# Scan over blocks of 128 tokens: factors of a block in one step, all its matmuls in the next, together with the decay sums of the following block

## The chip, the cores and the metric

The kernel is one program on one core of a Trainium2 chip. The metric is the device time of one execution in microseconds (us). A profile of one execution gives the rows that are shown below; its engines are PE (matmuls; PEld is its weight load), DVE (vector), ACT (activations), POOL (GpSimd) and SP (which issues most DMAs).

## What is computed

The reference is one layer of a hybrid model on 512 tokens of width 1024 and 16 leading meta tokens: two token mixers side by side (gated linear attention, and the state-space scan that is changed here), a gated merge, and a layer of retrieved experts. The scan, cut to what matters:

```
def ssd_chunk_step(S, inp):                       # one chunk of 64 tokens
    xdt, a, Bc, Cc = inp
    acum = jnp.cumsum(a, axis=1)
    seg = jnp.exp(-jnp.abs(acum[:, :, None] - acum[:, None, :]))
    cb = jnp.einsum('btgn,bsgn->btsg', Cc, Bc)
    y = jnp.einsum('btsgr,btsg,bsgrp->btgrp', seg, cb, xdt)
    y = y + jnp.einsum('btgn,bgrpn,btgr->btgrp', Cc, S, jnp.exp(acum))
    to_end = jnp.exp(acum[:, -1:] - acum)
    S = S * jnp.exp(acum[:, -1])[..., None, None] + jnp.einsum('bsgn,bsgr,bsgrp->bgrpn', Bc, to_end, xdt)
    return S, y
...
y = y + d_skip * xs_h;  y = y * jax.nn.silu(z);  y = rmsnorm(y per group of 512 channels)
```

The 2048 channels are four groups of 8 heads of 64. Each group has its own B and C, of 128 states.

## The kernel before

**Tiles.** A group g is scanned by the generator `sscan(g)` in four blocks i = 0 to 3 of 128 tokens, each of two chunks of 64 (A is the state at a block's start, B the state after its first chunk). Tiles are 128 partitions by 512, in float32. In a block the names are: `R`, the decay logarithms spread over a triangle (two POOL instructions); `pr`, their sums on PE (two matmuls); `sgm`, the factors seg times cb times dt, made of pr by DVE (subtract, then drop the sign bit), ACT (exp), DVE (times `cb`) and POOL (times `dt`); `py`, 16 small matmuls of `sgm` with the inputs `xs`; `xw`, the inputs times their decay to the chunk's end; `ssp`, a chunk's addition to the state (one matmul, rows 0 to 63 of `xw` for chunk A, 64 to 127 for B); `sS`, a state (POOL multiplies the old one by its decay, DVE adds `ssp`); `pi`, C times state, one matmul from A into output rows 0 to 63 and one from B into rows 64 to 127; `xd`, the inputs times d, to which DVE adds `py`; `y`, the block's output; `sy`, the sum of its squares (an ACT Square that uses `xd` as its bin); `ry`, the norm's factor (DVE, POOL). `turn` transposes a block's y on PE (`pyt`), copies it on ACT (`yt`) and stores it.

**What runs beside it.** `drive` advances two generators in turn. For g = 0 to 2 the other one is `sproj(g + 1)`, the projections of the next group: six units of 48 matmuls with 264 columns (called BT, CT, x0, x1, x2 and x3 here), each followed by a convolution on DVE (`cv`: four instructions), a tanh on ACT (`silu_t`) and a product on DVE, and then four units of 24 matmuls with 512 columns (z0 to z3). x0 to x3 are also transposed on PE (`px`, `pxm`) and copied by ACT (`xs`, `xsm`). For g = 3 the other one is `gates`, units of 24 matmuls with 512 columns (`pq`). Each unit's weights are split into a high part on ACT (`whi`) and a low part on DVE (`wlo`); three buffers of each rotate, so a split waits until the unit three places earlier is done. `sscan` has nine steps to sproj's ten.

**What sets the order.** The instructions of an engine stand in one row that a scheduler fixes when the program is built; each engine works its row off in that order, and a waiting instruction holds up all behind it. Tiles made by `mps` share four PSUM buffers in rotation: the fifth such tile waits until whoever reads the first has read it.

In PE's row of a group, block 0's matmuls stand behind x0, block 1's behind x2, block 2's behind z0 and block 3's behind z2. Of a block's two steps in the kernel before, the first makes R, pr and sgm up to the exp, and the second all the rest.

Of the kernel before, what the change touches and what calls it, by code (L numbers as in the profile page):

```python
# [6 lines left out]
F32 = mybir.dt.float32  # L7
F32R = mybir.dt.float32r
# [3 lines left out]
AF = mybir.ActivationFunctionType  # L12
OP = mybir.AluOpType
# [8 lines left out]
TT = 4  # L22
HL = L // 2
EPS = 1e-6
# [50 lines left out]
def body(tc, a, out):  # L75
# [3 lines left out]
    def act(o, i, f, **kw):  # L79
        S.activation(out=o, in_=i, func=f, **kw)  # L80

    def tt(eng, o, x, y, op):
        eng.tensor_tensor(o, x, y, op=op)  # L83
# [6 lines left out]
    with ExitStack() as top:  # L90
# [9 lines left out]
        def mps(name):  # L100
            return ps.tile([128, 512], F32, name=name, tag="m")
# [89 lines left out]
        def hv(x, c):  # L191
            return x.rearrange("p (h c) -> p h c", c=c)

        with ExitStack() as mix:
# [99 lines left out]
            def bc(x, g, n=128):  # L294
                return x[:, 8 * g:8 * g + 8, None].to_broadcast([n, 8, 64])
# [39 lines left out]
            def sscan(g):  # L335
                BT, CT, xs, xsm, zt = P_[g]

                p = mps("pcb")
                for i in range(TT):
                    for c in range(2):  # L340
                        t0 = NM + 128 * i + 64 * c
                        T.matmul(p[64 * c:64 * c + 64, 64 * i:64 * i + 64], BT[:, t0:t0 + 64], CT[:, t0:t0 + 64],
                                 start=True, stop=True)
                cb = sg.tile([128, TT, 64], F32, name="cb")
                act(cb, p[:, 0:256].rearrange("p (i c) -> p i c", c=64), AF.Copy, scale=0.25)
                p = mps("pbt")
                for i in range(TT):
                    T.transpose(p[:, 128 * i:128 * i + 128], BT[:, tok(i + 1)], ident)
                bt = sg.tile([128, TT, 128], F32, name="bt", bufs=2)
                act(bt, hv(p, 128), AF.Copy)  # L350
                p = mps("pbm")
                T.transpose(p[0:16, 0:128], BT[:, 0:16], ident)
                btm = sg.tile([16, 128], F32, name="btm", bufs=1)
                act(btm, p[0:16, 0:128], AF.Copy)

                def state(el, b_, xw, rows, old):
                    new = sg.tile([128, 512], F32, name="sS")
                    p = mps("ssp")
                    T.matmul(p, b_[rows], xw[rows], start=True, stop=True)
                    if old is None:  # L360
                        act(new, p, AF.Copy)
                    else:
                        tt(G, hv(new, 64), hv(old, 64), bc(el, g), OP.mult)
                        tt(V, new, new, p, OP.add)
                    return new

                y_ = []

                def turn(i, y):
                    p = mps("pyt")  # L370
                    for h in range(4):
                        T.transpose(p[:, 128 * h:128 * h + 128], y[:, 128 * h:128 * h + 128], ident)
                    yt = sg.tile([128, 512], F32, name="yt")
                    act(yt, p, AF.Copy)
                    nc.sync.dma_start(yT_d[:, 4 * g:4 * g + 4, 128 * i:128 * i + 128], hv(yt, 128))

                xwm = sg.tile([16, 512], F32, name="xwm", bufs=1)
                tt(V, hv(xwm, 64), hv(xsm, 64), bc(tdt[0:16, 0], g, 16), OP.mult)
                sA = state(None, btm, xwm, slice(0, 16), None)
                yield  # L380
                for i in range(TT):
                    R = sg.tile([128, 2, 512], F32R, name="R")
                    for e, z in enumerate((ath, atl)):
                        tt(G, hv(R[:, e], 64), tri64[:, None, :].to_broadcast([128, 8, 64]),
                           bc(z[:, i + 1].bitcast(F32), g), OP.mult)
                    pr = mps("pr")
                    T.matmul(pr, bdr, R[:, 0], start=True, stop=False)
                    T.matmul(pr, bdr, R[:, 1], start=False, stop=True)
                    sgm = sg.tile([128, 512], F32, name="sgm")
                    s8 = hv(sgm, 64)  # L390
                    tt(V, s8, hv(pr, 64), bc(ac[:, i], g), OP.subtract)
                    V.tensor_scalar(sgm.bitcast(I32), sgm.bitcast(I32), 0x7FFFFFFF, None, op0=OP.bitwise_and)
                    act(sgm, sgm, AF.Exp, scale=-1.0)
                    yield
                    if y_:
                        turn(*y_.pop())
                    tt(V, s8, s8, cb[:, i][:, None, :].to_broadcast([128, 8, 64]), OP.mult)
                    tt(G, s8, s8, bc(dt[:, i + 1], g), OP.mult)
                    xw = sg.tile([128, 512], F32, name="xw")
                    tt(G, hv(xw, 64), hv(xs[:, i], 64), bc(tdt[:, i + 1], g), OP.mult)  # L400
                    xd = sg.tile([128, 512], F32, name="xd")
                    tt(G, hv(xd, 64), hv(xs[:, i], 64), bc(dsk, g), OP.mult)
                    py = mps("py")
                    for h in range(8):
                        cs = slice(64 * h, 64 * h + 64)
                        for c in range(2):
                            rw = slice(64 * c, 64 * c + 64)
                            T.matmul(py[rw, cs], sgm[rw, cs], xs[rw, i, cs], start=True, stop=True)
                    sB = state(ex[:, i, 64:96], bt[:, i], xw, slice(0, 64), sA)
                    t0 = NM + 128 * i  # L410
                    pi = mps("pi")
                    T.matmul(pi[0:64], CT[:, t0:t0 + 64], sA, start=True, stop=True)
                    T.matmul(pi[64:128], CT[:, t0 + 64:t0 + 128], sB, start=True, stop=True)
                    sA = state(ex[:, i, 96:128], bt[:, i], xw, slice(64, 128), sB) if i < 3 else None
                    y = sg.tile([128, 512], F32, name="y")
                    tt(V, hv(y, 64), hv(pi, 64), bc(ex[:, i], g), OP.mult)
                    tt(V, xd, xd, py, OP.add)
                    tt(V, y, y, xd, OP.add)
                    tt(V, y, y, zt[:, i], OP.mult)
                    sy = sg.tile([128, 1], F32, name="sy")  # L420
                    act(xd, y, AF.Square, accum_out=sy)
                    ry = rstd(sg, sy, 1, 512, "ry", 4 * EPS)
                    V.tensor_scalar(y, y, ry, None, op0=OP.mult)
                    y_.append((i, y))
                    yield
                for z in y_:
                    turn(*z)

            def gates(n0, n1, pool, nb):
                for b in range(n0, n1):  # L430
# [722 lines left out]
```

## Time and profile before

| what | value |
|---|---|
| median of 3 runs | 2239.76 us (2239.16 to 2240.84) |
| the profiled execution's own time | 2239.76 us |
| its span (first to last instruction) | 2238.0 us |
| PE busy | 2124.1 us, 95% |
| DVE busy | 1571.6 us, 70% |
| granted share of PE's clock, mean | 0.977 |
| the scan stage | about 323 to 740 us of the span |

The span is the time between the program's first and last instruction, and 1.8 us of the time lie around it. A busy share is a mean over stages: what a change in the scan is worth is read from the scan's own rows.

### The profile page before, as it was taken

The page shows a single profiled execution, that of the slowest core. Times are in us where ns is not written, and L with a number is a line of the kernel's source. Part 1 is how long each engine was busy: PE and PEld are TensorE (multiplying, and loading weights), DVE is VectorE, ACT ScalarE, POOL GpSimd, SP SyncE. Part 2 cuts the span into 40 slices and gives each one's busy share as a digit, 9 for nine tenths or more (in the row PEclk, how much of TensorE's full clock was granted, in tenths as well). Part 3 has the DMA queues.
Part 4 walks back from the last instruction along what each step waited for, and adds up shares of the span by engine and source line. Part 5 has one row for each costly group of instructions (what it writes and reads, how often), then busy time and mean ns, then how long its engine had stood idle before and what let it go on. Part 6 is the DMA issues. An engine that isn't in the chain of part 4 may idle for free. (4 is left out here: it accounts for less than half of the span.)

```text
span 2238.0 us, 33023 instructions
## 1 busy us (share of the span) xinstructions
PE 2124.1 (95%) x12458; PEld 1834.8 (82%) x12458; DVE 1571.6 (70%) x2751; ACT 883.7 (39%) x1414; POOL 611.4 (27%) x564
## 2 busy tenths in 40 slices
PE   7988899998999999999999989999999999999997
PEld 6766677576766798988999978899988998899996
DVE  5374667575755466988999877877777777777775
ACT  5544433232322445445455532333333333333332
POOL 0253424433332000000000032433343434334331
PEclk9999999899899999999999999999999999999999
DMA  4557532121122778768857699988888888888883
GB/s 151 173 198 236 192 104 73 56 67 62 52 76 96 233 243 267 239 227 311 283 190 276 260 346 319 332 299 291 304 294 307 291 302 282 307 290 305 296 297 138
DMA packets 198432, 507.17 MB, mean 227 GB/s; under 512 B 16720, under 2 KB 89040, under 8 KB 196608
## 3 DMA queue, kind: packets, MB, share of 16 engines
q1 hardware_dynamic: 149440, 312.10, 41.4%
q0 software_dynamic: 48832, 192.96, 24.4%
q8 instruction: 97, 1.59, 0.3%
q14 instruction: 63, 0.52, 0.1%
HBM read 448.38 MB, written 56.62 MB: 226 GB/s over the span
## 5 line engine op out<-in xcount | busy, mean ns | idle before, releaser
L80 ACT ACTIVATE whi<-raw 128x1024 fp32r<-128x1024 f32 x433 | 458.7, 1060 | 536.1 <-PE pA L87 282.3
L83 DVE TENSOR_TENSOR wlo<-raw,whi 128x1024 fp32r<-128x1024 f32 x385 | 480.2, 1248 | 140.2 <-ACT whi L80 140.0
L86 PE MATMUL pA<-hh,whi 128*128 128x384 f32 x1024 | 346.4, 338 | 0.2 <-ACT ga L893 0.2
L88 PE MATMUL pA<-hh,wlo 128*128 128x384 f32 x1024 | 345.6, 338 | 0.4 <-DMA wlo<-lo_d 0.4
L87 PE MATMUL pA<-hl,whi 128*128 128x384 f32 x1024 | 345.8, 338 | 0.0
L969 POOL DMA_INDIRECT u<-in_pu,ix x128 | 172.5, 1348 | 301.3 <-ACT gh L1017 210.3
L983 DVE SCALAR_TENSOR_TENSOR hacc<-u,acg,hacc 128x1024 f32<-128x1024 f32 x128 | 164.7, 1286 | 116.2 <-DMA u<-in_pv,ix 115.5
L1030 PE MATMUL va<-wlo,gh 128*128 128x512 f32 x768 | 239.2, 393 | 7.5 <-DVE wlo L83 7.5
L969 POOL DMA_INDIRECT u<-in_pv,ix x128 | 168.4, 1316 | 282.8 <-ACT gh L1017 254.4
L1030 PE MATMUL va<-whi,gh 128*128 128x512 f32 x768 | 239.5, 394 | 5.5 <-ACT whi L80 5.5
L977 DVE SCALAR_TENSOR_TENSOR scr<-u,hg 128x1024 f32<-128x1024 f32 x128 | 156.6, 1224 | 98.0 <-DMA u<-in_pu,ix 97.2
L87 PEld LDWEIGHTS pA<-hl,whi 128*128 128x128 f32 x1024 | 192.6, 188 | 4.2
L86 PEld LDWEIGHTS pA<-hh,whi 128*128 128x128 f32 x1024 | 192.1, 188 | 4.0 <-ACT ga L893 0.3
L88 PEld LDWEIGHTS pA<-hh,wlo 128*128 128x128 f32 x1024 | 192.1, 188 | 0.6 <-DMA wlo<-lo_d 0.6
L1017 ACT ACTIVATE gh<-ga 128x384 fp32r<-128x384 f32 x128 | 67.2, 526 | 310.1 <-PE va L1030 301.0
L1030 PEld LDWEIGHTS va<-wlo,gh 128*128 128x128 f32 x768 | 144.9, 189 | 40.3 <-DVE wlo L83 9.6
L1030 PEld LDWEIGHTS va<-whi,gh 128*128 128x128 f32 x768 | 144.3, 190 | 28.9 <-ACT whi L80 5.8
L86 PE MATMUL pk<-whi,hh 128*128 128x512 f32 x256 | 104.7, 409 | 7.7 <-ACT vt L80 7.1
L88 PE MATMUL pya<-oyh,wlo 128*128 128x256 f32 x384 | 107.9, 281 | 0.0
L86 PE MATMUL pya<-oyh,whi 128*128 128x256 f32 x384 | 107.4, 280 | 0.0
L87 PE MATMUL pya<-oyl,whi 128*128 128x256 f32 x384 | 107.1, 279 | 0.0
L87 PE MATMUL pk<-wlo,hh 128*128 128x512 f32 x256 | 102.1, 399 | 0.0
(910 smaller groups left out, 4509.1 us busy)
## 6 DMA issues: line engine op xcount, KB each, us to landing
raw<-in_puT SPq DMA_DIRECT2D x128, 512.0 KB, 4.9
raw<-in_pv SPq DMA_DIRECT2D x128, 512.0 KB, 5.4
raw<-in_wup SPq DMA_DIRECT2D x48, 512.0 KB, 4.3
wlo<-lo_d SPq DMA_DIRECT2D x48, 512.0 KB, 4.8
W_d<-stg POOLq DMA_DIRECT2D x12, 2048.0 KB, 7.9
wb<-W_d SPq DMA_DIRECT2D x32, 768.0 KB, 8.7
lo_d<-zh POOLq DMA_DIRECT2D x64, 256.0 KB, 3.0
raw<-in_wpq SPq DMA_DIRECT2D x32, 512.0 KB, 5.2
```

What stands on the lines that cost most here:

```text
L80: S.activation(out=o, in_=i, func=f, **kw)
L83: eng.tensor_tensor(o, x, y, op=op)
L86: T.matmul(o, lh, rh, start=first, stop=False)
L87: T.matmul(o, lh, rl, start=False, stop=False)
L88: T.matmul(o, ll, rh, start=False, stop=last)
L969: g_ = G.indirect_dma_start(out=u, out_offset=None, in_=a[tab], in_offset=bass.IndirectOffsetOnAxis(ap=ix[:, i, k:k + 1], axis=0))
L977: V.scalar_tensor_tensor(scr, u, 1.0, hg[:, i], op0=OP.mult, op1=OP.mult, accum_out=ac_[:, k:k + 1])
L983: V.scalar_tensor_tensor(hacc[:, i], u, ac_[:, k:k + 1], hacc[:, i], op0=OP.mult, op1=OP.add)
L1017: i = S.activation(out=gh, in_=ga, func=AF.Copy)
L1030: T.matmul(va[t][c], x[:, cs], y[:, 512 * c:512 * c + 512], start=st_, stop=en_)
```

## The change

`state` is taken apart into `spsum` (the matmul) and `decay` (POOL's product). The step of a block is cut in another place. Its first step now norms the y of the block before (DVE), and makes sgm times cb (DVE), xw, the decayed state B, sgm times dt, the next block's R and xd (POOL). Its second step holds all matmuls: both `ssp`, `py`, both `pi`, the transposes of the block before and the `pr` of the next block, with what DVE and ACT make of them. R, sgm, xw, xd and yt have two buffers instead of three. The number of steps and of instructions is the same.

```
                 btm = sg.tile([16, 128], F32, name="btm", bufs=1)
                 act(btm, p[0:16, 0:128], AF.Copy)
 
-                def state(el, b_, xw, rows, old):
-                    new = sg.tile([128, 512], F32, name="sS")
+                def spsum(b_, xw, rows):
                     p = mps("ssp")
                     T.matmul(p, b_[rows], xw[rows], start=True, stop=True)
-                    if old is None:
-                        act(new, p, AF.Copy)
-                    else:
-                        tt(G, hv(new, 64), hv(old, 64), bc(el, g), OP.mult)
-                        tt(V, new, new, p, OP.add)
+                    return p
+
+                def decay(el, old):
+                    new = sg.tile([128, 512], F32, name="sS")
+                    tt(G, hv(new, 64), hv(old, 64), bc(el, g), OP.mult)
                     return new
-
-                y_ = []
 
                 def turn(i, y):
                     p = mps("pyt")
                     for h in range(4):
                         T.transpose(p[:, 128 * h:128 * h + 128], y[:, 128 * h:128 * h + 128], ident)
-                    yt = sg.tile([128, 512], F32, name="yt")
+                    yt = sg.tile([128, 512], F32, name="yt", bufs=2)
                     act(yt, p, AF.Copy)
                     nc.sync.dma_start(yT_d[:, 4 * g:4 * g + 4, 128 * i:128 * i + 128], hv(yt, 128))
 
-                xwm = sg.tile([16, 512], F32, name="xwm", bufs=1)
-                tt(V, hv(xwm, 64), hv(xsm, 64), bc(tdt[0:16, 0], g, 16), OP.mult)
-                sA = state(None, btm, xwm, slice(0, 16), None)
-                yield
-                for i in range(TT):
-                    R = sg.tile([128, 2, 512], F32R, name="R")
+                def spread(i):
+                    R = sg.tile([128, 2, 512], F32R, name="R", bufs=2)
                     for e, z in enumerate((ath, atl)):
                         tt(G, hv(R[:, e], 64), tri64[:, None, :].to_broadcast([128, 8, 64]),
                            bc(z[:, i + 1].bitcast(F32), g), OP.mult)
+                    return R
+
+                def decays(i, R):
                     pr = mps("pr")
                     T.matmul(pr, bdr, R[:, 0], start=True, stop=False)
                     T.matmul(pr, bdr, R[:, 1], start=False, stop=True)
-                    sgm = sg.tile([128, 512], F32, name="sgm")
-                    s8 = hv(sgm, 64)
-                    tt(V, s8, hv(pr, 64), bc(ac[:, i], g), OP.subtract)
+                    sgm = sg.tile([128, 512], F32, name="sgm", bufs=2)
+                    tt(V, hv(sgm, 64), hv(pr, 64), bc(ac[:, i], g), OP.subtract)
                     V.tensor_scalar(sgm.bitcast(I32), sgm.bitcast(I32), 0x7FFFFFFF, None, op0=OP.bitwise_and)
                     act(sgm, sgm, AF.Exp, scale=-1.0)
+                    return sgm
+
+                def norm(y, ry):
+                    V.tensor_scalar(y, y, ry, None, op0=OP.mult)
+
+                xwm = sg.tile([16, 512], F32, name="xwm", bufs=1)
+                tt(V, hv(xwm, 64), hv(xsm, 64), bc(tdt[0:16, 0], g, 16), OP.mult)
+                R = spread(0)
+                p = spsum(btm, xwm, slice(0, 16))
+                sA = sg.tile([128, 512], F32, name="sS")
+                act(sA, p, AF.Copy)
+                sgm = decays(0, R)
+                yield
+                yp = yq = None
+                for i in range(TT):
+                    s8 = hv(sgm, 64)
+                    if yp:
+                        norm(*yp[1:])
+                    tt(V, s8, s8, cb[:, i][:, None, :].to_broadcast([128, 8, 64]), OP.mult)
+                    xw = sg.tile([128, 512], F32, name="xw", bufs=2)
+                    tt(G, hv(xw, 64), hv(xs[:, i], 64), bc(tdt[:, i + 1], g), OP.mult)
+                    sB = decay(ex[:, i, 64:96], sA)
+                    tt(G, s8, s8, bc(dt[:, i + 1], g), OP.mult)
+                    if i < 3:
+                        R = spread(i + 1)
+                    xd = sg.tile([128, 512], F32, name="xd", bufs=2)
+                    tt(G, hv(xd, 64), hv(xs[:, i], 64), bc(dsk, g), OP.mult)
                     yield
-                    if y_:
-                        turn(*y_.pop())
-                    tt(V, s8, s8, cb[:, i][:, None, :].to_broadcast([128, 8, 64]), OP.mult)
-                    tt(G, s8, s8, bc(dt[:, i + 1], g), OP.mult)
-                    xw = sg.tile([128, 512], F32, name="xw")
-                    tt(G, hv(xw, 64), hv(xs[:, i], 64), bc(tdt[:, i + 1], g), OP.mult)
-                    xd = sg.tile([128, 512], F32, name="xd")
-                    tt(G, hv(xd, 64), hv(xs[:, i], 64), bc(dsk, g), OP.mult)
+                    pB = spsum(bt[:, i], xw, slice(0, 64))
+                    pA = spsum(bt[:, i], xw, slice(64, 128)) if i < 3 else None
+                    tt(V, sB, sB, pB, OP.add)
                     py = mps("py")
                     for h in range(8):
                         cs = slice(64 * h, 64 * h + 64)
                         for c in range(2):
                             rw = slice(64 * c, 64 * c + 64)
                             T.matmul(py[rw, cs], sgm[rw, cs], xs[rw, i, cs], start=True, stop=True)
-                    sB = state(ex[:, i, 64:96], bt[:, i], xw, slice(0, 64), sA)
+                    tt(V, xd, xd, py, OP.add)
                     t0 = NM + 128 * i
                     pi = mps("pi")
                     T.matmul(pi[0:64], CT[:, t0:t0 + 64], sA, start=True, stop=True)
                     T.matmul(pi[64:128], CT[:, t0 + 64:t0 + 128], sB, start=True, stop=True)
-                    sA = state(ex[:, i, 96:128], bt[:, i], xw, slice(64, 128), sB) if i < 3 else None
-                    y = sg.tile([128, 512], F32, name="y")
+                    if i < 3:
+                        sA = decay(ex[:, i, 96:128], sB)
+                        tt(V, sA, sA, pA, OP.add)
+                    y = sg.tile([128, 512], F32, name="y", bufs=3)
                     tt(V, hv(y, 64), hv(pi, 64), bc(ex[:, i], g), OP.mult)
-                    tt(V, xd, xd, py, OP.add)
                     tt(V, y, y, xd, OP.add)
                     tt(V, y, y, zt[:, i], OP.mult)
                     sy = sg.tile([128, 1], F32, name="sy")
                     act(xd, y, AF.Square, accum_out=sy)
-                    ry = rstd(sg, sy, 1, 512, "ry", 4 * EPS)
-                    V.tensor_scalar(y, y, ry, None, op0=OP.mult)
-                    y_.append((i, y))
+                    if yp:
+                        turn(*yp[:2])
+                    if i < 3:
+                        sgm = decays(i + 1, R)
+                    yp = (i, y, rstd(sg, sy, 1, 512, "ry", 4 * EPS))
                     yield
-                for z in y_:
-                    turn(*z)
+                norm(*yp[1:])
+                turn(*yp[:2])
 
             def gates(n0, n1, pool, nb):
                 for b in range(n0, n1):

```

What the scheduler makes of it shows in three places. The first is PE's row at block 1 of group 1, between unit x2 (before it) and unit x3 (behind it; L250, L251 and L253 are its matmuls). Before:

```order
L310 MATMUL px<-c_cst_79,xT 128x128 x4
L313 MATMUL pxm<-c_cst_79,xT 16x128
L372 MATMUL pyt<-c_cst_79,y 128x128 x4
L408 MATMUL py<-xs,sgm 64x64 x16
L250 MATMUL pa<-hh,whi 128x264
L251 MATMUL pa<-hl,whi 128x264
L250 MATMUL pb<-hh,whi 128x264
L359 MATMUL ssp<-xw,bt 128x512
L412 MATMUL pi<-sS,CT 64x512
L359 MATMUL ssp<-xw,bt 128x512
L251 MATMUL pb<-hl,whi 128x264
L413 MATMUL pi<-sS,CT 64x512
```

Now:

```order
L310 MATMUL px<-c_cst_79,xT 128x128 x4
L313 MATMUL pxm<-c_cst_79,xT 16x128
L358 MATMUL ssp<-xw,bt 128x512 x2
L425 MATMUL py<-xs,sgm 64x64 x16
L429 MATMUL pi<-sS,CT 64x512
L430 MATMUL pi<-sS,CT 64x512
L369 MATMUL pyt<-c_cst_79,y 128x128 x4
L383 MATMUL pr<-R,bdr 128x512
L384 MATMUL pr<-R,bdr 128x512
```

Both `ssp` stand together and ahead of `py`, both `pi` together behind it, the transposes of block 0 are `pyt` behind them, and the next block's `pr` is moved from the middle of the two units that follow to their front.

The second place is DVE's row at block 0 of group 1, from the end of the convolution of CT on. Before:

```order
L283 MEMSET rw 128x3
L279 SCALAR_TENSOR_TENSOR CT<-silu_t,cv 128x528
L287 TENSOR_SCALAR cv<-rw,c_cst_96 128x528
L83 TENSOR_TENSOR xd<-xd,py 128x512
L289 SCALAR_TENSOR_TENSOR cv<-rw,c_cst_96,cv 128x528
L83 TENSOR_TENSOR sS<-sS,ssp 128x512
L289 SCALAR_TENSOR_TENSOR cv<-rw,c_cst_96,cv 128x528
L83 TENSOR_TENSOR sS<-sS,ssp 128x512
L289 SCALAR_TENSOR_TENSOR cv<-rw,c_cst_96,cv 128x528
L83 TENSOR_TENSOR y<-pi,ex 128x512
L283 MEMSET rw 128x3
L83 TENSOR_TENSOR wlo<-raw,whi 128x1024
```

Now:

```order
L283 MEMSET rw 128x3
L279 SCALAR_TENSOR_TENSOR CT<-silu_t,cv 128x528
L83 TENSOR_TENSOR wlo<-raw,whi 128x1024
L287 TENSOR_SCALAR cv<-rw,c_cst_96 128x528
L83 TENSOR_TENSOR sS<-sS,ssp 128x512
L289 SCALAR_TENSOR_TENSOR cv<-rw,c_cst_96,cv 128x528
L83 TENSOR_TENSOR xd<-xd,py 128x512
L289 SCALAR_TENSOR_TENSOR cv<-rw,c_cst_96,cv 128x528
L83 TENSOR_TENSOR sS<-sS,ssp 128x512
L289 SCALAR_TENSOR_TENSOR cv<-rw,c_cst_96,cv 128x528
L83 TENSOR_TENSOR y<-pi,ex 128x512
```

The weight split `wlo` (for unit x3) and the first instruction of x0's convolution stand ahead of the first addition to the state, where before the split came behind the second one.

The third place is ACT's row at block 1 of group 1, up to the copies of the transposed inputs `xs` and `xsm`. Before:

```order
L80 ACTIVATE sgm<-sgm 128x512
L80 ACTIVATE whi<-raw 128x1024
L80 ACTIVATE silu_t<-cv 128x528
L80 ACTIVATE rw<-pa 128x264
L80 ACTIVATE rw<-pb 128x264
L80 ACTIVATE xs<-px 128x4x128
L80 ACTIVATE xsm<-pxm 16x128
L80 ACTIVATE yt<-pyt 128x512
```

Now:

```order
L80 ACTIVATE silu_t<-cv 128x528
L80 ACTIVATE whi<-raw 128x1024
L80 ACTIVATE rw<-pa 128x264
L80 ACTIVATE rw<-pb 128x264
L80 ACTIVATE xs<-px 128x4x128
L80 ACTIVATE xsm<-pxm 16x128
L80 ACTIVATE yt<-pyt 128x512
```

The exp of sgm has left this place, and the weight split `whi` has moved from ahead of the tanh `silu_t` to behind it.

## Rows read from the trace of the kernel before

**Rows 1.** The page: busy time by engine, and PE's granted clock in 40 equal slices of the span (tenths of full speed).

```profile
PE 2124.1 (95%) x12458; PEld 1834.8 (82%) x12458; DVE 1571.6 (70%) x2751; ACT 883.7 (39%) x1414; POOL 611.4 (27%) x564
...
PEclk9999999899899999999999999999999999999999
```

**Rows 2.** The waits from 323 to 740 us, the scan stage: who waited for whom, us in total, times, longest us.

```profile
PE py L408 <- POOL sgm L83: 26.2, 13, 4.4
...
DVE y L423 <- POOL ry L83: 14.5, 16, 1.5
```

**Rows 3.** Stretches of the scan stage: length, busy time of each engine with its count, PE's granted clock, DMA's share, GB/s.

```profile
388.20:402.50 14.30, 14.24 (x60) 7.43 (x61) 8.79 (x14) 2.80 (x8) 2.94 (x3) 0.52 0.18 57
432.40:450.50 18.10, 13.66 (x67) 7.74 (x67) 6.38 (x9) 2.49 (x5) 6.90 (x7) 0.81 0.15 43
...
472.10:494.50 22.40, 18.70 (x148) 15.04 (x147) 18.88 (x29) 7.57 (x15) 10.16 (x9) 1.00 0.14 48
494.50:508.50 14.00, 13.99 (x95) 10.13 (x96) 9.38 (x16) 3.80 (x10) 3.49 (x3) 0.88 0.21 57
...
596.20:610.70 14.50, 14.50 (x62) 7.69 (x63) 8.85 (x14) 2.77 (x8) 3.17 (x3) 0.53 0.20 55
...
640.40:660.00 19.60, 15.16 (x72) 8.90 (x73) 7.08 (x10) 3.88 (x7) 6.92 (x7) 0.83 0.14 41
660.00:735.00 75.00, 74.58 (x413) 51.02 (x412) 36.84 (x50) 23.31 (x39) 18.59 (x18) 1.00 0.34 110
```

**Rows 4.** The timeline at the first matmuls of groups 0, 1 and 2 (`pcb`): start, us, engine, line, operation.

```profile
351.10 0.69 PE L342 MATMUL pcb<-CT,BT 128*64 128x64 f32 x16
...
457.37 0.69 PE L342 MATMUL pcb<-CT,BT 128*64 128x64 f32 x16
...
559.04 0.69 PE L342 MATMUL pcb<-CT,BT 128*64 128x64 f32 x16
```

**Rows 5.** The timeline of PE in group 1 from the last matmul of x0, over block 0 and block 1, to the matmuls of x3; in brackets the idle time before and what ended it.

```profile
471.86 0.28 PE L253 MATMUL pb<-hh,wlo 128*128 128x264 f32 x1
473.09 1.15 PE L408 MATMUL py<-xs,sgm 64*64 64x64 f32 x32 [0.94 <-POOL sgm L83]
474.17 1.12 PE L359 MATMUL ssp<-xw,bt 64*128 64x512 f32 x2
475.22 1.07 PE L412 MATMUL pi<-sS,CT 128*64 128x512 f32 x2
476.22 1.12 PE L359 MATMUL ssp<-xw,bt 64*128 64x512 f32 x2
...
494.51 1.88 PE L408 MATMUL py<-xs,sgm 64*64 64x64 f32 x32 [2.64 <-POOL sgm L83]
...
502.08 0.39 PE L253 MATMUL pa<-hh,wlo 128*128 128x264 f32 x1
```

**Rows 6.** The timeline of ACT at block 1 and block 2 of group 1.

```profile
490.68 1.06 ACT L80 ACTIVATE whi<-raw 128x1024 fp32r<-128x1024 f32 x1 [0.23 <-PE pb L251]
493.65 0.64 ACT L80 ACTIVATE silu_t<-cv 128x528 f32<-128x528 f32 x1 [1.91 <-DVE cv L289]
...
494.74 0.60 ACT L80 ACTIVATE xs<-px 128x512 f32<-128x512 f32 x1
...
516.56 0.58 ACT L80 ACTIVATE xs<-px 128x512 f32<-128x512 f32 x1
```

**Rows 7.** The timeline of PE in group 1 behind x3, and at blocks 2 and 3: the first transposes and pr, z0, the start of z1, and the py and a matmul of z3 at block 3.

```profile
507.56 0.60 PE L310 MATMUL px<-c_cst,xT 128*128 128x128 f32 x4
...
508.02 0.47 PE L387 MATMUL pr<-R,bdr 128*128 128x512 f32 x1
...
508.56 0.39 PE L86 MATMUL pk<-whi,hh 128*128 128x512 f32 x1
...
514.14 0.60 PE L310 MATMUL px<-c_cst,xT 128*128 128x128 f32 x4
...
515.93 1.15 PE L408 MATMUL py<-xs,sgm 64*64 64x64 f32 x32 [0.65 <-POOL sgm L83]
...
521.22 0.50 PE L86 MATMUL pk<-whi,hh 128*128 128x512 f32 x1
...
538.40 1.49 PE L408 MATMUL py<-xs,sgm 64*64 64x64 f32 x32 [4.39 <-POOL sgm L83]
...
546.35 0.50 PE L88 MATMUL pk<-whi,hl 128*128 128x512 f32 x1
```

**Rows 8.** The timeline of PE in the attention scan, far ahead of the stage that is changed: the sums of two chunks, rows 0 to 63 and rows 64 to 127, in eight passes of 256 columns.

```profile
268.67 1.14 PE L549 MATMUL gsp<-vt,kd 64*128 64x256 f32 x8
```

**Rows 9.** Groups of instructions from 323 to 740 us: line, engine, operation, names, shapes, count; busy us, mean ns of one; idle us before them and who ended it.

```profile
L83 DVE TENSOR_TENSOR wlo<-raw,whi 128x1024 fp32r<-128x1024 f32 x44 | 61.0, 1387 | 39.6 <-ACT whi L80 39.5
L289 DVE SCALAR_TENSOR_TENSOR cv<-rw,c_cst,cv 128x528 f32<-128x528 f32 x57 | 48.6, 853 | 0.5
L83 DVE TENSOR_TENSOR sS<-sS,ssp 128x512 f32<-128x512 f32 x28 | 19.2, 684 | 18.6 <-PE ssp L359 14.9 <-POOL sS L83 3.7
L287 DVE TENSOR_SCALAR cv<-rw,c_cst 128x528 f32<-128x528 f32 x19 | 17.0, 896 | 0.0
...
L83 POOL TENSOR_TENSOR xd<-xs,dsk 128x512 f32<-128x512 f32 x16 | 24.2, 1511 | 31.6 <-ACT xd L80 31.6
L83 POOL TENSOR_TENSOR sgm<-sgm,dt 128x512 f32<-128x512 f32 x16 | 20.8, 1299 | 43.1 <-DVE sgm L83 43.1
```

## The prediction

> **What bounds the kernel now.** I began with the page. PE is busy for 95% of the span, and its granted clock is below nine tenths in two slices alone, the eighth and the eleventh [rows 1]. The clock has two levels, 2.4 and 1.2 GHz, so such a slice is a mixture. Both slices (392 to 448 and 560 to 615 us) lie in the scan stage, and all that follows is read there. The waits of the stage [rows 2] show one long wait of PE: for the factors that POOL multiplies into sgm, 26.2 us in 13 times. PE's timeline in group 1 [rows 5, 7] says where: 0.94 us at block 0, 2.64 at block 1, 0.65 at block 2, 4.39 at block 3. Elsewhere in groups 0 to 2 PE goes from matmul to matmul.
>
> The stretches [rows 3] show the second loss. In group 0 (388.2 to 402.5) the clock is at 0.52 after block 1, in group 1 (494.5 to 508.5) at 0.88, in group 2 (596.2 to 610.7) at 0.53; a mean of 0.52 over 14.3 us is 13.7 us at the lower level, so the three are 13.7, 3.4 and 13.6. Behind block 3 it is 0.81 over 18.1 us and 0.83 over 19.6 (the first and the last of three such stretches), 6.8 us each. Together some 51 us, each time right behind a wait of 2.6 or 4.4 us. Group 3, from 660 to 735, holds the same matmuls without such a wait, and its clock is 1.00. What a us at the lower level costs is read from the groups' first matmuls [rows 4]: group 0 takes 106.27 us and group 1 101.67. They differ by 4.6 us in time and by 10.3 us of low clock, so 0.45 us per us; all 51 us cost 23.
>
> So a clean pipeline could gain 26 + 23 = 49 us and more. The question is what stands behind the wait that goes.
>
> **The change, part by part.** Nothing is added or taken away: the same instructions stand in another order. I cost it by group, from the end of x0 (471.98 in group 1, the last matmul starting at 471.86 and 0.12 being a start-to-start step there) [rows 5].
>
> *The factors.* pr now stands ahead of two units (about 11.5 us) instead of one, and its R is made a block earlier. The chain pr, DVE, ACT, DVE, POOL, some 8 us with what stands between, is covered. The wait for sgm goes, everywhere.
>
> *Block 0.* The two ssp stand together, one on rows 0 to 63, one on rows 64 to 127. The nearest row is the attention scan's sum [rows 8]: eight passes of 256 columns, half of them on either set of rows, take 1.14 us, as long as the two passes of 512 that one ssp needs [rows 5]; that is twice the columns in the time. I take 1.05 us for a pair of ssp, where two cost 2.1. Bounds: 1.05 and 2.1. py is 1.08 (473.09 to 474.17) and one pi 1.0 (475.22 to 476.22). So pi from state A ends 3.1 us after x0. The pi from state B needs DVE's addition, and DVE's row has wlo and x0's first cv ahead of it. That wlo needs whi, which starts behind the tanh of CT: 0.64 + 1.06 us [rows 6], so DVE starts at 1.8, and wlo 1.39, cv 0.90 and the addition 0.68 [rows 9] end at 4.8. PE waits about 1.8 us. Bounds: nothing, if CT's convolution is early, and 2.5. pi ends at 5.8.
>
> *Block 1.* pr is 0.54 us (508.02 to 508.56) [rows 7], x1 and x2 11.8 (96 steps of 0.123), px and pxm 0.46, the ssp pair 1.05. PE could begin py at 19.8. But py is the fifth PSUM tile from px on, and must wait for ACT to copy xs. In ACT's row the copy stands behind the tanh of x1, which needs x1's convolution from DVE. What DVE does up to there: in the kernel before it was busy for 18.9 us between 472.1 and 494.5 [rows 3]; less the two of CT that are done earlier now it is about 17. It starts at 1.8 and waits 0.9 for the norm's factor (14.5 us over 16) [rows 2] and some 0.3 for a whi, so x1's convolution ends at 20.0 (before, at 21.7: the tanh starts at 493.65 [rows 6]). Then tanh 0.6, whi 1.06, two copies 0.55 and xs 0.6: py begins at 22.9, a wait of 3.1 us. Bounds 1.5 and 4.5. Before, py began 22.5 us after x0. So the factors come in time, and the transposed inputs don't. With py 1.08, two pi 2.0, pyt 0.44 (as px) and pr 0.54, x3 begins at 27.0. Before, it ran on from 502.08 with four matmuls done, as if begun at 501.6: 29.6 after x0, or 28.1 without the 1.5 that low clock took. Gain 1.1.
>
> *Block 2.* Before, x3's and z0's stretch up to z1 (521.22) [rows 7] took 19.6. Now: x3 5.9, px 0.46, z0 5.6 (508.56 to 514.14), px 0.46, ssp pair 1.05, and PE is at py 7.6 us after x3. xs was copied 9.6 us after x3 (516.56 + 0.58, x3 ending at 507.56) [rows 6, 7], by a chain that the change leaves as it is: a wait of 2.0, bounds 0 and 3. Then 1.08 + 2.0 + 0.44 + 0.54. Sum 19.5, gain 0.1.
>
> *Block 3.* Before, z3 ran on from 546.35 with two matmuls done, as if from 545.9: 24.7 after z1's start, 21.6 without 3.1 for low clock. DVE has no convolution here, and nothing of what PE needs is late: 5.6 + 0.46 + 5.6 + 1.05 + 1.08 + 2.0 + 0.44 = 16.2. Gain 5.4.
>
> Per group 6.6, three groups 19.8. *Group 3* has no waits, but three ssp pairs at 1.05 less (3.2) and four pi pairs, on separate output rows. A pi pair could halve too, by up to 1.0; B's state comes about when A's pi begins, so I take half: 5.0 in all, bounds 0 and 7.
>
> *Clock.* Behind block 3 the wait is gone: 20.4 us at the lower level, 9.2 us of time. Behind block 1 a wait of 3.1 takes the place of 2.6, and the clock will fall there again; I take 6.8 us each time, as behind block 3, in place of 30.7 in all: 10.3 less, 4.6 us. The waits of 1.8 and 2.0 us lie between 0.94, after which it didn't fall, and 2.64, after which it did. I count no fall; each costs 3.1 if it comes.
>
> Sum: 19.8 + 5.0 + 9.2 + 4.6 = 38.6 from 2239.76: **2201 us** (the profiled execution's time is the median). Own range with the bounds above, 2190 to 2212.
>
> *Work that must stay hidden.* Each wlo is made up to two units (11 us) ahead, so a few us on DVE cost PE nothing as long as the split is at most that late. The norm and turn of a block lie a step later with 11 us of cover. pr's buffer after block 0 needs py's and the states' additions, done while pi runs.
>
> **The rivals.**
> *A clean pipeline (0.20).* DVE and ACT are quicker than I count, PE waits nowhere, and its clock stays. Gains 6.6 + 1.8 + 3.1 + 2.0 per group, 5.0 and 23: 2170; with half of the waits, 2185. For it: DVE is idle for 30% of the span [rows 1]. Against it: DVE's 18.9 of 22.4 us at block 1.
>
> The Trainium skill (SBUF — State Buffer, "SBUF: two separate sides") says that a POOL instruction and a DVE instruction with two SBUF inputs exclude each other for their whole length. In the stretch at block 1 DVE's 18.9 us, less five instructions that read PSUM (3.4), and POOL's 10.2 [rows 3] make 25.7, waiting for each other counted in; by that rule the stretch hardly shrinks below 22, which is an estimate, and a clean pipeline, which needs 17, is not to be had. By it the sum would be that of the next rival.
>
> *DVE and POOL hold each other up (0.17).* The chains at blocks 1 and 2 end 1.6 us later than I count (DVE's and POOL's busy times add up to 29.0 in 22.4 us, so they overlap little): 3 x 3.2 = 9.6, or 2211; if the clock also falls behind blocks 0 and 2, six times 3.1, 2224 to 2229.
>
> *No change that can be measured (0.05).* The waits for xs and the states are those of before in other clothes, and the clock falls as before: only block 3's 5.4 a group would be left, and eaten by 2 to 3 us at block 0 and 2: about 2236.
>
> *Slower (0.03).* POOL's row takes the place: sgm times dt of block i+1 stands behind xd, which waits for the Square of block i, and behind ry. From pi's end the chain is seven DVE instructions (4.8 us), xd 1.5, ry 0.55, sgm 1.3 [rows 9], 8.2 us against 13 us of matmuls. It would cost only from 13 us on; to lose 43 us (38.6 and 0.2%) at nine blocks it must wait about 1.7 us each and bring 3.1 us of clock each time, a chain twice as long as the rows give. 2245 or more.
>
> **How the numbers follow.** My case has 0.55. A difference of 0.2% (4.5 us) is about what a measurement of this kernel tells from none. Faster 0.92, same 0.05, slower 0.03. The range reaches to 2177, halfway into the clean pipeline, and to 2222, into the rival with more falls of the clock.
>
> **What would show it.** Right: no wait of PE for POOL's sgm over 1 us in groups 0 to 2; py of block 1 waiting 1.5 to 4.5 us for ACT's xs; pi of block 0 waiting 0 to 2.5 us for DVE's sS; no wait at block 3, and full clock behind it; the two ssp within 1.2 us; groups of about 90 to 95 us. Wrong: the scan stage's clock full throughout and groups near 85 us (clean), a PE wait for wlo, or py again waiting for sgm.

## The result, and the profile after

The changed kernel takes 2185.99 us (median of 4 runs, 2182.43 to 2189.25) where the kernel before takes 2240.05 (4 runs beside it): ratio 0.9745 [0.9721, 0.9769], 54 us faster. The forecast was 2201, with 2177 to 2222 as its range: the direction and the range hold, the gain is 15 us larger than forecast. The profiled execution took 2189.25 us, its span is 2187.5. Four single executions among the runs below took 2728 to 11658 us and count in no ratio and no median here.

The page's row of the granted clock and the waits of PE from 323 to 740 us (answering to [rows 1, 2]), and the first matmuls of the groups (to [rows 4]):

```profile
PEclk9999999999999999999999999999999999999999
...
PE py L425 <- ACT xsm L80: 12.6, 6, 2.9
PE pi L430 <- DVE sS L83: 4.0, 3, 1.3
...
351.29 0.69 PE L342 MATMUL pcb<-CT,BT 128*64 128x64 f32 x16
439.88 0.69 PE L342 MATMUL pcb<-CT,BT 128*64 128x64 f32 x16
528.58 0.69 PE L342 MATMUL pcb<-CT,BT 128*64 128x64 f32 x16
615.94 0.69 PE L342 MATMUL pcb<-CT,BT 128*64 128x64 f32 x16
```

No wait for POOL's sgm is left. For the scan's tiles PE waits 16.6 us in the stage instead of 26.2, and for others: ACT's copies of the transposed x (py) and DVE's state (pi). The groups take 88.6, 88.7 and 87.4 us, where they took 106.3, 101.7 and 105.3.

PE's timeline in group 1 at blocks 0 to 3 (answering to [rows 5, 7]), and ACT's at block 1 (to [rows 6]):

```profile
454.39 0.28 PE L253 MATMUL pb<-hh,wlo 128*128 128x264 f32 x1
454.61 1.13 PE L358 MATMUL ssp<-xw,bt 64*128 64x512 f32 x4
455.67 1.15 PE L425 MATMUL py<-xs,sgm 64*64 64x64 f32 x32
456.75 1.07 PE L429 MATMUL pi<-sS,CT 128*64 128x512 f32 x2
459.16 1.07 PE L430 MATMUL pi<-sS,CT 128*64 128x512 f32 x2 [1.34 <-DVE sS L83]
...
472.46 0.60 PE L310 MATMUL px<-c_cst,xT 128*128 128x128 f32 x4
473.10 1.13 PE L358 MATMUL ssp<-xw,bt 64*128 64x512 f32 x4
477.09 1.15 PE L425 MATMUL py<-xs,sgm 64*64 64x64 f32 x32 [2.86 <-ACT xsm L80]
...
478.17 1.12 PE L429 MATMUL pi<-sS,CT 128*64 128x512 f32 x1
...
480.18 0.69 PE L369 MATMUL pyt<-c_cst,y 128*128 128x128 f32 x2
...
496.90 1.15 PE L425 MATMUL py<-xs,sgm 64*64 64x64 f32 x32 [1.33 <-ACT xsm L80]
497.98 0.64 PE L429 MATMUL pi<-sS,CT 128*64 128x512 f32 x1
...
499.19 0.66 PE L369 MATMUL pyt<-c_cst,y 128*128 128x128 f32 x4
...
514.00 0.64 PE L429 MATMUL pi<-sS,CT 128*64 128x512 f32 x1
514.01 0.64 PE L430 MATMUL pi<-sS,CT 128*64 128x512 f32 x1
514.48 0.59 PE L429 MATMUL pi<-sS,CT 128*64 128x512 f32 x1
514.49 0.59 PE L430 MATMUL pi<-sS,CT 128*64 128x512 f32 x1
515.01 0.66 PE L369 MATMUL pyt<-c_cst,y 128*128 128x128 f32 x4
...
474.31 0.64 ACT L80 ACTIVATE silu_t<-cv 128x528 f32<-128x528 f32 x1 [5.32 <-DVE cv L289]
474.86 1.04 ACT L80 ACTIVATE whi<-raw 128x1024 fp32r<-128x1024 f32 x1
...
476.35 0.60 ACT L80 ACTIVATE xs<-px 128x512 f32<-128x512 f32 x1
476.83 0.25 ACT L80 ACTIVATE xsm<-pxm 16x128 f32<-16x128 f32 x1
```

A float32 matmul of 512 columns shows as two passes in PE's row. Two ssp, four passes, take 1.13 us; before, the two passes of one took 1.12. At block 3 the passes of the two pi start 0.01 us apart. At block 1 py waits for the copies that stand in ACT's row behind the tanh, which waits for DVE's convolution: the chain that the prediction named.

The three stretches of group 0, 1 and 2 in which the clock was below its upper level, and the stage from group 3 on (answering to [rows 3]):

```profile
389.40:392.80 3.40, 3.40 (x17) 1.67 (x13) 3.40 (x6) 0.09 (x1) 1.44 (x1) 0.50 0.43 154
478.20:481.60 3.40, 3.40 (x12) 1.69 (x11) 3.40 (x7) 0.27 (x1) 1.44 (x1) 0.50 0.43 149
566.90:570.30 3.40, 3.40 (x11) 1.69 (x11) 3.40 (x7) 0.29 (x1) 1.44 (x1) 0.50 0.42 149
616.00:723.00 107.00, 105.55 (x566) 78.29 (x566) 52.91 (x74) 39.85 (x66) 24.22 (x23) 1.00 0.48 159
```

The 1.2 GHz level holds for 10.2 us, each time behind block 1's wait, where it held for some 51.

### The profile page after: what moved, and what is told of

It reads as the page before. It is cut to its first block, busy times and chain, and to the rows that moved or that the text cites. A ratio compares the mean times of both kernels' runs of the same rounds, so it can differ in the third digit from the quotient of the medians.

```text
span 2187.5 us, 33055 instructions
## 1 busy us (share of the span) xinstructions
PE 2083.8 (95%) x12458; PEld 1825.2 (83%) x12458; DVE 1584.0 (72%) x2751; ACT 884.0 (40%) x1414; POOL 607.6 (28%) x564
## 5 line engine op out<-in xcount | busy, mean ns | idle before, releaser
L88 PE MATMUL pk<-whi,hl 128*128 128x512 f32 x256 | 102.3, 399 | 0.0
```

What stands on the lines that cost most here:

```text
L88: T.matmul(o, ll, rh, start=False, stop=last)
```

## The experiments

Ratios are to the kernel before on the same chip, with a 95% interval; 0.001 of a ratio is 2.2 us. "Three groups" is the time from the first pcb of group 0 to that of group 3 in each trace. The two don't always say the same: on the later chips the kernel before took 2235 to 2252 us with mean granted clocks of 0.971 to 0.978, where the one trace of it stands at 2239.76 and 0.977, so a ratio may also hold some clock that this trace doesn't show.

| kernel | ratio [95%] | three groups, us |
|---|---|---|
| before | 1 | 313.2 |
| before, two buffers for xw and xd | 0.9911 [0.9883, 0.9940] | 300.9 |
| before, pairs | 0.9827 [0.9801, 0.9854] | 287.6 |
| before, pairs and two buffers | 0.9827 [0.9797, 0.9856] | 280.6 |
| after, late sums, three buffers | 0.9829 [0.9803, 0.9855] | 280.3 |
| after, late sums | 0.9763 [0.9728, 0.9797] | 271.1 |
| after, pairs undone | 0.9815 [0.9777, 0.9854] | 277.9 |
| after, three buffers | 0.9754 [0.9732, 0.9776] | 261.8 |
| after | 0.9745 [0.9721, 0.9769] | 264.7 |
| after, on a second chip | 0.9755 [0.9730, 0.9779] | 264.8 |
| after, px first | 0.9767 [0.9736, 0.9798] | 264.2 |
| after, norm on ACT | 0.9723 [0.9685, 0.9761] | 259.5 |
| after, px first and norm on ACT | 0.9747 [0.9723, 0.9771] | 260.3 |
| after, norm and first tap on ACT | 0.9727 [0.9707, 0.9748] | 259.9 |

**Pairs undone in the changed kernel.**

```
-pB = spsum(.., 0:64); pA = spsum(.., 64:128); sB += pB; py; xd += py; pi from sA; pi from sB
+py; pB = spsum(.., 0:64); sB += pB; xd += py; pi from sA; pA = spsum(.., 64:128); pi from sB
```

> The changed kernel with the old order of a block's matmuls (py, ssp, pi, ssp, pi) and all else as changed, the early pr too. Theory (two ssp on separate rows and two pi on separate output rows run at the same time): in group 3 each of three ssp pairs and four pi pairs costs about 1.0 us more, 5 to 7 us; in groups 0 to 2 blocks 0 to 2 wait for DVE and ACT anyway, so about 3 us a group; 2186 + 14 = about 2200 us, no wait for POOL's sgm. Rival (a pair is no quicker than two apart, the whole gain is the early pr): 2186 within 4 us.

2204.3 us, ratio 0.9815: by ratio 13 to 16 us over the changed kernel (0.9745, 0.9755). In the traces it is 13 in the three groups and 4.5 from group 3's pcb to the end of the stage's last projection (626.11 to 737.67, in the changed kernel 615.94 to 722.99). Some 4.6 of the 13 are clock, since the lower level holds for 20.5 us in the groups instead of 10.2. That is what the pairs are worth where everything else is changed; the pairs theory holds.

**Decay sums one unit ahead again.** decays(i) and, a unit later, cb and dt stand where they did; R, the pairs and the two buffers stay.

```
-if i < 3: sgm = decays(i + 1, R)          # end of step i
+sgm = decays(i, R)                        # first half of step i; cb and dt in the second
```

> The changed kernel with pr, the exp and the products with cb and dt back where they were (pr one unit ahead of py instead of two), the pairs of matmuls kept. Theory (the early pr removes the wait for sgm and with it the falls of the clock): the waits for POOL's sgm come back with about 2.5 us at block 1 and 4 us at block 3, the clock falls behind both, about 50 us of low clock; 2240 less the 5 us of group 3 and some 3 us a group from the pairs, about 2225 us. Rival (the pairs and the earlier norm bring most of it): 2200 us or less, sgm waits below 1 us.

2194.8: the rival. PE waits for sgm 2.4 us in all, 0.8 at the longest, beside 16.3 for the copies and xw, where the changed kernel has 12.6 for the copies. So the prediction's account of what removes the 4.39 us at block 3 was incomplete. The end of sgm on DVE at block 3 of group 1 and POOL's rows there, first in the kernel before, then POOL's in this one:

```profile
532.79 0.67 DVE L83 TENSOR_TENSOR sgm<-sgm,cb 128x512 f32<-128x512 f32 x1
...
529.09 2.04 POOL L83 TENSOR_TENSOR R<-c_cst,atl 128x512 fp32r<-128x512 f32 x1
531.09 1.22 POOL L83 TENSOR_TENSOR xw<-xs,tdt 128x512 f32<-128x512 f32 x1
532.28 2.09 POOL L83 TENSOR_TENSOR xd<-xs,dsk 128x512 f32<-128x512 f32 x1
534.33 1.04 POOL L83 TENSOR_TENSOR xw<-xs,tdt 128x512 f32<-128x512 f32 x1
535.33 2.02 POOL L83 TENSOR_TENSOR xd<-xs,dsk 128x512 f32<-128x512 f32 x1
537.31 1.04 POOL L83 TENSOR_TENSOR sgm<-sgm,dt 128x512 f32<-128x512 f32 x1
```

```profile
510.85 1.22 POOL L83 TENSOR_TENSOR xw<-xs,tdt 128x512 f32<-128x512 f32 x1
512.03 2.09 POOL L83 TENSOR_TENSOR xd<-xs,dsk 128x512 f32<-128x512 f32 x1
514.09 1.04 POOL L83 TENSOR_TENSOR sgm<-sgm,dt 128x512 f32<-128x512 f32 x1
515.09 2.08 POOL L83 TENSOR_TENSOR xw<-xs,tdt 128x512 f32<-128x512 f32 x1
```

In the kernel before, DVE was done with sgm at 533.46 (532.79 + 0.67), but POOL was at the first of two pairs of xw and xd until 534.33 and made the second, too, before sgm. Both are for the next group (counted through the group, its own four pairs had been made). The scheduler seems to put them there as soon as their inputs and a buffer are free; the change gives xw and xd two buffers, and with late sums one pair is left ahead. The next three runs test that.

**Before, with two buffers for xw and xd alone.**

```
-xw = sg.tile([128, 512], F32, name="xw")           # three buffers; xd alike
+xw = sg.tile([128, 512], F32, name="xw", bufs=2)
```

> The kernel before with one edit: xw and xd have two buffers each instead of three. Nothing else is changed in the code. In the trace of before, block 3's sgm times dt (537.31 in group 1) stood on POOL behind two pairs of xw and xd (531.09 to 537.31), of which one is not needed before the next group; with two buffers only one pair can be made ahead of it. Theory (block 3's wait was POOL's row, and buffers let it grow): the multiplication starts some 3.1 us earlier, py at block 3 waits about 1.3 us instead of 4.4, and the clock does not fall behind it; three groups by 3.1 us of wait and 6.8 us of low clock at 0.45 give 18.5 us: about 2221 where before takes 2240, 0.9917 of it. Rival (the wait comes from the chain pr, DVE, ACT, DVE, POOL that begins too late, whatever stands between): the wait at block 3 stays above 3 us and the time within 5 us of before.

0.9911, 20 us by ratio (13 to 26), but 12.4 in the three groups, where 18.5 were expected. Block 3's wait is 1.41 us, the waits for sgm add up to 17.0, and behind block 3 the clock fell in one group of three, for 3.4 us. So the theory holds for block 3, except that both pairs of before are the next group's, not one. The rest went behind block 1 of group 1: there the lower level holds for 13.7 us instead of 3.4, behind the same wait (2.65 us, before 2.64). Its PE at block 3:

```profile
530.19 1.15 PE L408 MATMUL py<-xs,sgm 64*64 64x64 f32 x32 [1.41 <-POOL sgm L83]
```

**Late sums with three buffers, and the changed kernel with three.** The same edit the other way, in two kernels.

> The kernel with late sums (decay sums one unit ahead, pairs kept), and xw and xd with three buffers instead of two. POOL's row at block 3 then has two pairs of xw and xd ahead of sgm times dt, as the kernel before had. Theory (the buffers hid the cost of the late sums): the wait at block 3 grows from 1.4 to about 4.5 us and the clock falls behind it, 3 x (3.1 + 3.1) = 18.6 us more than the kernel with late sums and two buffers: ratio to before about 0.985 instead of 0.9763. Rival (the early norm and the step order cured block 3): within 4 us of the late sums with two buffers, ratio 0.975 to 0.978.

> The changed kernel with xw and xd in three buffers instead of two. The sums are early, so sgm times dt of block 3 stands ahead of the pairs of the next group on POOL. Theory (early sums or two buffers, either of them cures block 3): the same time as the changed kernel, within 3 us, no wait for sgm at block 3. Rival (the two buffers are the whole cure): a wait of 3 us or more at block 3 comes back, with the clock's fall 18 us slower.

Both theories hold. With late sums the third buffer costs 15 us by ratio (9 in the three groups): the wait for sgm is back at block 3, with 6.8 us at the lower level behind it in groups 0 and 2, 3.4 in group 1:

```profile
523.31 1.59 PE L425 MATMUL py<-xs,sgm 64*64 64x64 f32 x32 [3.81 <-POOL sgm L83]
```

With early sums the third buffer costs nothing (0.9754 against 0.9755). So either of the two edits cures block 3 (two buffers with late sums leave 0.8 us of wait there), and the early sums are worth 17 us with three buffers, but only some 2 to 4 (6 in the three groups) with two.

> The changed kernel itself, beside these on one chip, for the comparison: 2182 to 2189 us if the chip is as the first one; the ratio to before 0.972 to 0.977.

It is 2187.8, ratio 0.9755.

**Pairs alone, and pairs with two buffers, in the kernel before.**

```
+pB = spsum(bt[:, i], xw, slice(0, 64)); pA = spsum(bt[:, i], xw, slice(64, 128))
 py; pi from sA; pi from sB                # the ssp between them gone
```

> The kernel before with one edit: the two ssp of a block stand together ahead of py, and the two pi together behind it; buffers, decay sums and all else as before. Theory (a pair takes half the time of two): behind py there stand 2.1 to 3.1 us of matmuls instead of 5.2; at a block that waits for sgm the ssp pair, now ahead of py, fills 1.05 us of the wait. That is 7 to 11 us a group in groups 0 to 2 and 5 in group 3, less 0.8 us a group at block 1, where py now waits for ACT's xs: 24 to 36, about 2210, ratio 0.987. Rival (in groups 0 to 2 the times are set by DVE, ACT and POOL, and the pairs only make PE wait longer): 5 us in group 3 and little else, 2230 or more, ratio above 0.995.

> The kernel before with the pairs (as in the kernel with the pairs alone) and with two buffers for xw and xd (as in the kernel with two buffers alone), nothing else. Theory (pairs and POOL's row are nearly all of the change's gain, and add up): the gain of the pairs and 15 to 18 us for block 3, about 2192 to 2200, ratio 0.978 to 0.982. Rival (without the early sums the gains eat each other, since a shorter block leaves the chain of the factors less time): less than 10 us better than the pairs alone, ratio above 0.983.

The pairs alone give 39 us by ratio (33 to 45) and 32 in the traces of the stage (25.7 in the three groups, 6.4 behind them): the upper part of what I gave them (24 to 36), or more. With the two buffers the wait for sgm goes from 10.0 to 1.1 us in the stage, but the medians move by 2 us (2206.7 to 2204.9) and the three groups by 7: the rival, which said less than 10. The trace shows where a part goes: an ssp waits for ACT's xs, 13.4 us instead of 10.4. In this order pyt stands ahead of the ssp pair, so the fifth PSUM tile from px on is the second ssp; in the changed kernel pyt stands behind pi, and it is py, a matmul later:

```profile
475.22 0.60 PE L310 MATMUL px<-c_cst,xT 128*128 128x128 f32 x4
475.66 0.27 PE L313 MATMUL pxm<-c_cst,xT 128*16 128x128 f32 x1
475.77 0.60 PE L375 MATMUL pyt<-c_cst,y 128*128 128x128 f32 x4
476.30 1.12 PE L358 MATMUL ssp<-xw,bt 64*128 64x512 f32 x2
480.53 1.26 PE L358 MATMUL ssp<-xw,bt 64*128 64x512 f32 x2 [2.31 <-ACT xs L80]
```

The kernel with late sums has pairs and two buffers too, and the new order of the steps beside them: 0.9763 against 0.9827. What part of these 14 us is the place of pyt, what the earlier work on POOL and DVE, and what the two buffers of R, sgm and yt, wasn't separated.

**What holds the changed kernel up.** px ahead of the unit, so that ACT can copy earlier; the norm of y on ACT instead of DVE; both; the norm and the convolution's first tap on ACT.

```
-if b < 4: conv(..) else: next(z_)         # px first: these two lines
-if b >= XLAG: turn(..)                    # change places
...
-V.tensor_scalar(y, y, ry, None, op0=OP.mult)
+act(y, y, AF.Copy, scale=ry)              # norm on ACT
...
-V.tensor_scalar(cv, rw[:, 0:L], convw[:, b, 0:1], convb[:, b:b + 1], op0=OP.mult, op1=OP.add)
+act(cv, rw[:, 0:L], AF.Identity, scale=convw[:, b, 0:1], bias=convb[:, b:b + 1])   # first tap
```

> The changed kernel with the transposes of the next group's inputs (px, pxm) ahead of a projection unit instead of behind it, so that ACT's copies xs and xsm are done long before py needs their PSUM buffers. Theory (DVE's row is what is late at blocks 0 to 2): PE's wait for ACT's xsm goes (12.6 us in the changed kernel) but pi waits for DVE's addition to the state instead, 2 us at block 1 and 1 us at block 2; the time stays within 4 us of 2186. Rival (the rotation of the PSUM buffers and ACT's copy are what is late): 4.2 us a group and the clock's three falls go, 12.6 + 4.6 us, about 2169 us.

> The changed kernel with the norm's product y times ry on ACT instead of DVE. Theory (DVE's row is what is late): DVE loses 0.5 to 0.6 us and a wait for ry of 0.5 to 0.9 us between block 0 and block 1, so x1's convolution ends about 1 us earlier, py's wait at block 1 falls from 2.9 to about 1.9 us and that of block 2 by about 0.7; if the clock no longer falls behind block 1, 1.5 us more per group; 2176 to 2182 us. Rival (ACT's row is what is late, and gets 0.6 us more per block): 2186 or slower, up to 2192 us.

> The changed kernel with both earlier edits: px ahead of the unit, and the norm of y on ACT instead of DVE. Theory (DVE's row is what is left: px first alone only moved the wait of block 1 from ACT's xs to DVE's sS, and a shorter row of DVE then pays): faster than the changed kernel by 10 to 18 us, ratio to before 0.967 to 0.971. Rival (the waits for sS at blocks 2 and 3 stay and eat the gain): as with px first alone, ratio 0.974 to 0.977.

> The kernel with the norm on ACT, and the convolution's first tap (cv from rw, 0.66 us on DVE, six a group) on ACT as well. Theory (what is left of waits in groups 0 to 2, 2.0 us at block 1 and 1.3 at block 0 in the kernel with the norm on ACT, is the length of DVE's row): DVE's row up to block 1 is 1.3 us shorter (x1 and x2), ACT's 0.6 to 1.2 us longer; py at block 1 waits 0.5 to 1.5 us, groups of 85 to 86.5 us, the clock stays at its upper level through the stage; ratio to before 0.967 to 0.971, against 0.9723 with the norm alone. Rival (ACT's row, on which the transposed copies stand, becomes the bound): block 1's wait for ACT is 2 us or more, ratio 0.972 to 0.977.

PE's waits in the stage with px first, with the norm on ACT, and with norm and tap on ACT:

```profile
PE pi L430 <- DVE sS L83: 10.6, 9, 2.0
PE pr L383 <- DVE sS L83: 3.3, 3, 1.1
PE px L310 <- DVE xT L279: 3.0, 1, 3.0
```

```profile
PE py L425 <- ACT xsm L80: 7.5, 6, 2.0
PE pi L430 <- DVE sS L83: 4.0, 3, 1.3
```

```profile
PE py L425 <- ACT xs L80: 6.4, 3, 2.2
PE py L425 <- ACT xsm L80: 3.1, 3, 1.0
```

With px first no wait for the copies is left and the clock doesn't fall in the groups, yet they take as long as in the changed kernel: the wait has moved to DVE's states, as the DVE theory said. Ahead of group 0, outside the three groups, this order costs a wait of 3.0 us more, for DVE's xT. With the norm's 0.7 us a block gone from DVE the copies' wait falls from 12.6 to 7.5 us and the three groups by 5 us. With the tap on ACT as well, pi no longer waits, but py waits up to 2.2 us for ACT, and a matmul of the projections waits for another copy of ACT (rw, 2.1 us in all): the rival there, and no further gain. Both edits together were no better than the norm alone. The two kernels with work on ACT and px in its old place have the lowest ratios, 0.9723 and 0.9727 against 0.9745 and 0.9755, but the intervals overlap: 0.2 to 0.3% better is likely, not settled.

## Why the prediction was right, and where it was short

*Right, step by step.* No wait for sgm; py of block 1 waits 2.86 us for ACT's copies (predicted 3.1, between 1.5 and 4.5); pi of block 0 waits 1.34 for DVE's state (1.8, up to 2.5); py of block 2 waits 1.33 (2.0); no wait at block 3, and no fall of the clock there; the ssp pair 1.06 us from its start to that of py (454.61 to 455.67; 1.05). From x0's end to the end of x1's convolution it was 19.7 us (454.39 + 0.12 to DVE's last cv, 471.85 + 2.37), predicted 20.0. Group 3 and what of the stage stands behind it gained 5.2 us (5.0). Slips in the working move none of this by more than 0.2 us: 1.70 is written as 1.8 (DVE's start at block 0), 19.65 as 19.8 and 22.81 as 22.9 (block 1), 5.2 as 5.0 (group 3). By its own terms the clean pipeline with half of the waits would be 2182, not 2185.

*The terms that were too small.* Groups 0 to 2 gained 48.6 us; the sum had 33.6.

- The clock: 41 us less at the lower level by 0.45 is 18.4, predicted 13.8. I took 6.8 us behind each of block 1's waits; it was 3.4. Short by 4.6. The rows couldn't give this size: in the kernel before the same wait of 2.64 us, with the same matmuls behind it, was followed by 13.7, 3.4 and 13.6 us.
- The waits: 5.5 us a group in group 1, predicted 6.9. Short by 1.4 a group, 4.1.
- The pi pairs: I gave them nothing in groups 0 to 2. From the first pi to pyt it takes 2.0 us at block 1 (478.17 to 480.18, at the lower level), 1.2 at block 2 (497.98 to 499.19), 1.0 at block 3 (514.00 to 515.01), where I counted 2.0 each. Short by 1.8 a group, 5.4.

That is 14.1 of 15.0. The "groups of about 90 to 95 us" were wrong for the same reasons. At the end of the stage's last projection 53.6 us are gained (776.6 to 723.0), in the profiled span 50.5: 3.1 us were lost in later stages, which hold the same instructions. The profiled execution is the slowest of its four, which spread over 6.8 us, and the medians are 54 us apart: whether anything is lost there, these runs don't tell.

*The step that was right in its result and wrong in its reason.* "The chain is covered. The wait for sgm goes, everywhere": it went, but the largest of these waits, block 3's, was mostly POOL's row (1.41 of its 4.39 us stay when a buffer of xw and xd is taken away and nothing else), not the chain's late start. Early sums cure it because they put sgm ahead of the next group's pairs in that row: in the changed kernel with three buffers POOL makes it at 501.52 and two pairs from 503.79 on. The prediction looked at POOL's row for what the change could put ahead of sgm, and not for what stood there before; that the diff also takes a buffer from xw and xd it didn't count at all. With two buffers, early sums hardly matter. And the parts don't add: by ratio 39 us for the pairs in the kernel before and some 15 in the changed kernel, 20 for the buffers alone and almost nothing beside the pairs (in the three groups 12 and 7). A part of what each wins is given back at the next row, ACT's copies and DVE's states.

*The rivals.* The clean pipeline (2170) didn't come about; its nearest kernel, with the norm on ACT, still waits at block 1. DVE and POOL holding each other up (2211 and more) didn't either. In this stretch of the changed kernel (group 1, x0's end to block 1; columns as in [rows 3]) their busy times add up to 31.1 us in 22.0, so the records overlap by 9 us at least:

```profile
455.00:477.00 22.00, 17.89 (x147) 14.33 (x143) 20.13 (x27) 7.57 (x16) 11.00 (x9) 1.00 0.14 49
```

That is no proof that both worked at once: DVE's wlo takes 2.09 us at 455.95 and 1.23 at 475.93, so a busy time may hold time in which an engine was kept waiting.

The Trainium skill's exclusive lock (SBUF — State Buffer, "SBUF: two separate sides") led to an estimate that the stretch at block 1 hardly shrinks below 22 us. In the changed kernel it took 22.6 (454.51 to 477.09), but with px first 19.6 (457.64, the start of block 0's ssp, to py at 477.19): the measurement decides against the estimate as a floor for PE's stretch. There part of DVE's work fell behind it, where pi then waited, so whether, and for how long, POOL and DVE keep each other out is not shown.

The Trainium skill (TensorEngine Tiling (Array Packing), "Key Properties") says that different tiles can run their matmuls in parallel; the pairs agree, 1.13 us for the work that took 2.2.

## What to carry to other kernels

Before you explain a wait by a chain's length, read the row of the engine that releases it: what ran just ahead of the late instruction, and who needs that? A buffer more can let a scheduler put early work there, and a buffer less can be the cure. Matmuls on separate rows or columns of the array belong next to each other; that alone was worth 32 to 39 us here, and it asks for no new data flow. Gains of parts overlap where the next wait is close behind: measure each part in both the old and the new surroundings.

## What the runs showed of the hardware that I had not expected

- Two matmuls of 512 columns on separate output columns of the array, next to each other in the program, run side by side: at block 3 their passes start 0.01 us apart and the pair takes 1.0 us, as long as one alone. I had counted half of that gain at most.
- The clock's stay at the lower level isn't set by the wait alone. Behind 2.64 us at block 1 it was 13.7, 3.4 and 13.6 us in groups 0, 1 and 2 of the kernel before, and the matmuls that follow are the same in all three. With two buffers for xw and xd, behind 2.6 us, it was 13.7 three times; in the changed kernel, behind 2.83 to 2.88 us, 3.4 three times. What decides was not tested.
